# Two layers of a hybrid diffusion backbone on one core: who makes the first weight sums, where squares and spills lie, and where the modulation is computed

## The chip, the cores and the metric

The kernel runs on one core of one Trainium2 chip. The metric is device time in microseconds, as the median of several executions. The engines are TensorE (PE in the rows; its weight loads PEld), VectorE (DVE), ScalarE (ACT), GpSimd (POOL) and SyncE (SP), whose queue issues nearly all DMAs. Each engine executes its own instructions in program order, and waits for others by semaphores.

## The reference

Two layers with shared weights run over 1024 latent tokens and 256 context tokens, 1024 channels wide. Each layer does

```
mod        = silu(cond) @ w_mod[l] + b_mod[l]         # six vectors: sh1 sc1 g1 sh2 sc2 g2, per token group
h          = rms_norm(x, norm_mix[l]) * (1 + sc1) + sh1
x          = x + g1 * (mixer(h) @ w_out)              # layer 0: neighbourhood attention and pooling
                                                      # layer 1: windowed grouped-query attention
h          = rms_norm(x, norm_ffn[l]) * (1 + sc2) + sh2
gu         = h @ w_gate_up[l]
x          = x + g2 * ((silu(gu[:2816]) * gu[2816:]) @ w_down[l])
```

and a final RMSNorm follows. All of it is float32.

## The kernel before

Tokens are columns, channels are partitions. There are three blocks of columns, `TB`: ti = 0 and 1 with 512 latent tokens each, ti = 2 with the 256 prompt tokens. A float32 operand is split into two parts, a high one and the rest, and a product is three matmuls (high x high, high x rest, rest x high; L308 to L310 in `dense`, L863 to L865 in `prod`, L1032 to L1034 in `mix`). So every weight tile (`whl`, L281 copy on ScalarE, L283 subtraction) and every activation is made in two parts.

**Queue order.** The order of work is the order of the program text. Side work is put in by hand: `bg` is a list of tasks, and `bg.step(n)` issues the next n of them (a task that returns true ends the step early); `bg.need(key)` issues all up to a key. `W.done(i)` issues the making of weight unit i + 4. `md.step()` issues one step of a modulation job: eight steps are a tile of `w_mod` each (L387, L389, two products on VectorE), then two empty ones, two sums over partitions (L401, transposes on PE, and L402), and one that adds the bias. `Mod` keeps `bufs` tiles loaded ahead on SP's queue.

**Stages.** Input projection of layer 0 (up to 301 us in the trace) with modulation jobs (0, 4) to (0, 9) among it and `md.all()` at its end; attention; `out_proj`; `ffn(0)`; input projection of layer 1; attention; `out_proj`; `ffn(1)`.

**FFN.** It has 22 units (128 hidden channels each). The two latent blocks go through a seven-product scheme on 512 x 512 halves: weights G (gate) and U (up) of a unit give four weight tiles G, A, B, U, where A and B are made of sums and differences of half tiles (`make`, L272 to L276, on GpSimd), and activations give seven operands Q11, Q21, Q22, T1 to T4 (`norm_parts`). The prompt block uses plain `dense`: `prompt_gate` and `up_prompt`. Units 0 and 1 are interleaved in `begin`, since T1 to T4 are still being made there; the others are `front`, `prompt_gate`, `back`. A unit's result is split in two parts and spilled to DRAM (`spill`, tile x2_1, `hd`). Then `down(q)` goes through six groups of hidden channels (2, 4, 4, 4, 4, 4 units): `load_h` brings their spilled parts back, `mix` multiplies and adds into the residual `x` (L1036), which `load_x` has brought back from `xr`. The last group also squares the new residual and sums the squares (`Norm.feed`, ScalarE L426 into tile s2, sum L427 on GpSimd), and `tail` puts the next norm's tasks in `bg`.

**Start of the FFN.** In `out_proj` the second half (g = 1) writes the residual (L817), feeds the norm sums, and steps `bg` with the norm tasks of the block before. `norm_parts` makes the operands: `alloc` and `finish_a` (sum over partitions on PE, L433, root and reciprocal, L435 and L436), `finish_b` (L442), then, for ti = 0 and 2, `apply` (L485, L488, L491) and for ti = 1 the tasks of Q22 and T1 to T4 (L502, L503, L517, L530, L534). GpSimd or VectorE does the subtraction in `two` (L503).

## Time and profile before

| | us |
|---|---|
| median of 3 runs | 3140.95 (3139.73 to 3142.19) |
| the profiled execution | 3142.91 |
| its span, first to last instruction | 3141.1 |
| mean granted TensorE clock | 0.965 |
| PE busy | 2939.9 (94%) |
| VectorE busy | 1853.1 (59%) |
| ScalarE busy | 1090.4 (35%) |
| GpSimd busy | 852.4 (27%) |

Busy time is the time in which an engine's instructions were executing, so a PE at half clock is busy for twice as long with the same work. A wait is put down to the instruction that released it. Times in the rows are counted from the first instruction of the span.

### The profile page before, as it was taken

What the parts mean: (1) busy time and instruction counts of PE and PEld (TensorE: products, weight loads), DVE (VectorE), ACT (ScalarE), POOL (GpSimd) and SP (SyncE); (2) the same over time, 40 slices, a digit from 0 to 9 for tenths busy, and PEclk for the clock granted to TensorE, in tenths of its full rate; (3) what the DMA queues carried; (4) which work ended last, traced back from release to release, by engine and by line L of the source; (5) the groups of instructions that cost most, each with busy time, mean ns of one, the idle gap of its engine ahead of it and who ended that gap; (6) DMA issues with size and microseconds to landing.
All of it is one profiled execution on the core that took longest, in us unless ns stands there. A gap on an engine that the chain in (4) does not pass through costs nothing.

```text
span 3141.1 us, 46254 instructions
## 1 busy us (share of the span) xinstructions
PE 2939.9 (94%) x18074; PEld 2489.3 (79%) x18074; DVE 1853.1 (59%) x3007; ACT 1090.4 (35%) x2084; POOL 852.4 (27%) x720
## 2 busy tenths in 40 slices
PE   6998999969999998799989999999699999999998
PEld 4877777858888887688778778778588888888887
DVE  5655665567777777554445688872655555544334
ACT  4232674232333332000233477761433333330002
POOL 0340452233333332000222344430333343320002
PEclk9999999979999999899989999999799999999999
DMA  6458736204343445634224411123022223245421
GB/s 240 151 188 254 172 80 195 93 26 134 128 134 131 128 131 198 227 131 181 73 89 158 151 56 47 35 64 112 27 97 91 91 91 100 105 164 208 175 101 68
DMA packets 184330, 394.55 MB, mean 126 GB/s; under 512 B 32176, under 2 KB 69424, under 8 KB 177840
## 3 DMA queue, kind: packets, MB, share of 16 engines
q1 hardware_dynamic: 180656, 385.34, 36.4%
q0 software_dynamic: 3456, 6.26, 0.8%
q8 instruction: 143, 2.34, 0.3%
q14 instruction: 75, 0.61, 0.1%
HBM read 274.32 MB, written 118.23 MB: 125 GB/s over the span
## 4 chain that ended last, share of the span: by engine, by line
PE 74%; DVE 10%; ACT 5%; POOL 4%; issue 3%; DMA 3%; SPq 0%; POOLq 0%; DVEq 0%; ACTq 0%
PE psd L309 8%; PE psd L308 8%; PE psd L310 8%; PE psd L863 6%; PE psd L864 6%; PE psd L865 6%; PE psd L1032 6%; PE psd L1033 6%; PE psd L1034 6%; PE ps_t L672 5%; PE ps_o L688 4%; PE ps_s L620 4%; DVE nacc L389 2%; ACT whl L281 1%; ACT sT L677 1%
## 5 line engine op out<-in xcount | busy, mean ns | idle before, releaser
L308 PE MATMUL psd<-A,whl 128*128 128x256 f32 (+1 forms) x1760 | 586.3, 333 | 8.6 <-ACT whl L281 3.3
L309 PE MATMUL psd<-A,whl 128*128 128x256 f32 (+1 forms) x1760 | 580.9, 330 | 9.9 <-DVE A L491 9.5
L310 PE MATMUL psd<-A,whl 128*128 128x256 f32 (+1 forms) x1760 | 578.8, 329 | 1.6 <-DVE whl L283 1.6
L281 ACT ACTIVATE whl<-wraw 128x1024 fp32r<-128x1024 f32 x178 | 187.5, 1055 | 665.0 <-PE psd L1034 479.6
L1032 PE MATMUL psd<-A,whl 128*128 128x512 f32 (+1 forms) x1056 | 378.6, 359 | 30.9 <-DVE x L1036 30.8
L1033 PE MATMUL psd<-A,whl 128*128 128x512 f32 (+1 forms) x1056 | 376.0, 356 | 0.0
L1034 PE MATMUL psd<-A,whl 128*128 128x512 f32 (+1 forms) x1056 | 375.9, 356 | 0.0
L309 PEld LDWEIGHTS psd<-A,whl 128*128 128x128 f32 x1760 | 338.4, 192 | 45.5 <-DVE A L491 11.0
L308 PEld LDWEIGHTS psd<-A,whl 128*128 128x128 f32 x1760 | 338.1, 192 | 43.2 <-ACT whl L281 4.1
L310 PEld LDWEIGHTS psd<-A,whl 128*128 128x128 f32 x1760 | 342.1, 194 | 31.3 <-DVE whl L283 2.9
L1036 DVE SCALAR_TENSOR_TENSOR x<-psd,modv,x 128x512 f32<-128x512 f32 (+1 forms) x288 | 187.7, 661 | 300.8 <-PE psd L1034 283.8
L283 DVE TENSOR_TENSOR whl<-wraw,whl 128x1024 fp32r<-128x1024 f32 x174 | 235.8, 1358 | 145.5 <-ACT whl L281 143.0
L427 POOL TENSOR_TENSOR nacc<-nacc,s 128x512 f32<-128x512 f32 (+1 forms) x78 | 89.4, 1147 | 837.0 <-ACT s L426 833.7
L863 PE MATMUL psd<-A,whl 128*128 128x512 f32 x704 | 279.4, 397 | 0.0
L865 PE MATMUL psd<-A,whl 128*128 128x512 f32 x704 | 277.4, 394 | 0.0
L864 PE MATMUL psd<-A,whl 128*128 128x512 f32 x704 | 277.3, 394 | 0.0
L1032 PEld LDWEIGHTS psd<-A,whl 128*128 128x128 f32 x1056 | 201.0, 190 | 61.2 <-DVE x L1036 33.4
L662 POOL TENSOR_SCALAR sP<-sP,sm 128x896 f32<-128x896 f32 (+2 forms) x206 | 180.2, 879 | 244.7 <-DVE sm L655 118.1
L1034 PEld LDWEIGHTS psd<-A,whl 128*128 128x128 f32 x1056 | 202.1, 191 | 28.1
L1033 PEld LDWEIGHTS psd<-A,whl 128*128 128x128 f32 x1056 | 201.1, 190 | 27.5
L672 PE MATMUL ps_t<-ident,sP 128*128 128x128 f32 x1408 | 207.3, 286 | 6.2 <-POOL sP L662 2.6
L672 PEld LDWEIGHTS ps_t<-ident,sP 128*128 128x128 f32 x1408 | 153.3, 143 | 56.4 <-issue 24.9
(212 smaller groups left out, 5210.4 us busy)
## 6 DMA issues: line engine op xcount, KB each, us to landing
hd<-x SPq DMA_DIRECT2D x88, 512.0 KB, 3.1
A<-hd SPq DMA_DIRECT2D x20, 2048.0 KB, 11.0
wraw<-in_w_gu_dram SPq DMA_DIRECT2D x60, 512.0 KB, 3.6
st<-in_w_mod_dram SPq DMA_DIRECT2D x96, 256.0 KB, 2.8
wraw<-in_w_down_dram SPq DMA_DIRECT2D x44, 512.0 KB, 3.7
wmod<-in_w_mod_dram SPq DMA_DIRECT2D x64, 256.0 KB, 3.0
wrawx<-in_w_gu_dram SPq DMA_DIRECT2D x28, 512.0 KB, 3.7
A<-hd SPq DMA_DIRECT2D x14, 1024.0 KB, 15.0
```

The source lines that it names most:

```text
L281: act.activation(h[:, 0], src, AF.Copy)
L283: eng.tensor_tensor(h[:, 1], src, h[:, 0].bitcast(F32), op=OP.subtract)
L308: pe.matmul(ps[:, :n], wh, A[ti].part(0, k), start=(k == 0), stop=False)
L309: pe.matmul(ps[:, :n], wh, A[ti].part(1, k), start=False, stop=False)
L310: pe.matmul(ps[:, :n], wl, A[ti].part(0, k), start=False, stop=(k == 7))
L672: pe.transpose(pt[:, 128 * (i - lo):128 * (i - lo) + 128], P[u][:, 128 * j:128 * j + 128], ident)
L863: pe.matmul(pt, wh, t(0, c), start=(c == 0), stop=False)
L864: pe.matmul(pt, wh, t(1, c), start=False, stop=False)
L865: pe.matmul(pt, wl, t(0, c), start=False, stop=(c == 3))
L1032: pe.matmul(pt[:, :n], wh, t[:, 0, k], start=(k == 0), stop=False)
L1033: pe.matmul(pt[:, :n], wh, t[:, 1, k], start=False, stop=False)
L1034: pe.matmul(pt[:, :n], wl, t[:, 0, k], start=False, stop=(k == nk - 1))
```

## The change

Nine edits, in the order of the diff:

- `padl` and most of `ones` go, and one slab gets a longer pad.
- `make`: units up to number 13 (A and B of the first two units of an FFN) take their sums on VectorE, the rest stays on GpSimd.
- `Norm.feed`: a square can lie in a tile that the caller names. `squares` names the tiles ea and ec of the pool gq, in `out_proj` (blocks 1 and 2) and in the last group of `down`.
- `norm_parts`: a subtraction that VectorE does is issued behind the next task (`lagged`), and an empty task follows each kind.
- `out_proj`: with g = 1 only the first two of the prompt block's steps call `W.done`; `md` steps also for g = 1, ti = 0; three tasks per step rather than four; another interleaving of what is left with the prompt block's norm tasks. `begin` splits units 10 and 11 after each `front` and steps `bg` by 3 after each `prompt_gate`.
- The last unit spills into tiles wrawx and T2, takes T4's product (`c21`) ahead of Q22's, loads block 0's residual right behind it, and block 2's ahead of its `prompt_gate`. The first group of `down` takes the blocks in the order 2, 1, 0.
- The last two of the eight sums of squares in the last group go to VectorE.
- Modulation: the input projection of layer 0 keeps jobs (0, 4) to (0, 7); (0, 8) and (0, 9) move to `out_proj`, (0, 10) and (0, 11) from there to `ffn(0)`, (1, 10) and (1, 11) from `ffn(0)` to `ffn(1)`, which had none.
- The norm tasks behind `ffn(0)` get 4, 7 and 0 empty tasks in front rather than 1 each.

```diff
@@ make
-            g = self.raw.get(r)
+            g, add = self.raw.get(r), dve if self.ns < 14 else pool
...
-                pool.tensor_tensor(src[:, 512:1024], u[:, 0:512], u[:, 512:1024], op=OP.add)
-                pool.tensor_tensor(src[:, 0:512], g[:, 0:512], src[:, 512:1024], op=OP.subtract)
+                add.tensor_tensor(src[:, 512:1024], u[:, 0:512], u[:, 512:1024], op=OP.add)
+                add.tensor_tensor(src[:, 0:512], g[:, 0:512], src[:, 512:1024], op=OP.subtract)
...
@@ Norm
-        def feed(self, xc, eng=pool):
+        def feed(self, xc, eng=pool, square=None):
...
-                s = npool.tile([128, 512], F32, name="s2", bufs=3)
+                s = square() if square else npool.tile([128, 512], F32, name="s2", bufs=3)
...
@@ norm_parts
+        late = []
+        def lagged(f):
+            prev = late[:]
+            del late[:]
+            f()
+            for g in prev:
+                g()
         def two(hi, lo, src, eng=pool):
             act.activation(hi, src, AF.Copy)
-            eng.tensor_tensor(lo, src, hi.bitcast(F32), op=OP.subtract)
+            f = lambda: eng.tensor_tensor(lo, src, hi.bitcast(F32), op=OP.subtract)
+            late.append(f) if eng is dve else f()
...
@@ out_proj
+    def squares(gq):
+        n = [0]
+        def f():
+            n[0] += 1
+            return gq.tile([128, 512], F32, name=("ea", "ec")[n[0] % 2], bufs=2)
+        return f
...
-                    if ti == 2:
+                    if ti == 2 and (g == 0 or j < 2):
                         W.done(wi)
-                    if md is not None and g == 0:
+                    if md is not None and (g == 0 or ti == 0):
...
-                    bg.step((5, 5, 4 if j else 1)[ti])
+                    bg.step((5, 5, 3 if j else 1)[ti])
...
-                        bg.q = t[:1] + q[:1] + t[1:2] + q[1:2]
-                        q, t = q[2:], t[2:]
+                        bg.q = q[:1] + t[:1] + q[1:3] + t[1:2]
+                        q, t = q[3:], t[2:]
                         while q or t:
-                            bg.q += t[:2] + q[:1]
+                            bg.q += q[:1] + t[:2]
@@ ffn
         def spill(i, ti, src):
-            h = xp.tile([128, 2, 512], F32R, name="x2_1")
+            if i < NHC - 1:
+                h = xp.tile([128, 2, 512], F32R, name="x2_1")
+            elif ti == 0:
+                h = gq.tile([128, 2, 512], F32R, name="wrawx")
+            else:
+                h = gq.tile([128, 2, 4, 512], F32R, name="T2")[:, :, 0]
...
             for i in range(2):
                 front(i, S[i])
+                W.split(10 + i)
             for i in range(2):
                 prompt_gate(i, S[i])
+                bg.step(3)
...
             if last:
                 load_x(1)
+            if last:
+                c21(i, s, uw, v)
+                load_x(0)
             m = prod(w, 512, "Q22")
...
-                        for ti in range(3):
+                        for ti in ((0, 1, 2) if q else (2, 1, 0)):
                             mix(q, m + k, ti, w, 128 * GROUPS[q] * k, None)
...
-                nm.feed(xc)
+                nm.feed(xc, pool if m < 6 else dve, sq)
...
                 load_h(0, 1)
+                load_x(2)
...
-        load_x(0)
-        load_x(2)
...
-    md = Mod(st_pool, [(0, j) for j in range(4, 10)], 4)
+    md = Mod(st_pool, [(0, j) for j in range(4, 8)], 4)
...
-    md = Mod(mp, [(0, 10), (0, 11)], 3, mp)
+    md = Mod(mp, [(0, 8), (0, 9)], 3, mp)
...
-    md = [(1, j) for j in range(12)]
+    md = [(0, 10), (0, 11)] + [(1, j) for j in range(10)]
...
-        norm_tasks(nm, lambda c: xt[ti][c], 1, 0, ti, A1, (1, 1))
+        norm_tasks(nm, lambda c: xt[ti][c], 1, 0, ti, A1, ((4, 1), (7, 1), (0, 1))[ti])
...
-    ffn(W, 1, xt, A, g2, tail1, None, xr)
+    ffn(W, 1, xt, A, g2, tail1, [(1, 10), (1, 11)], xr)
```

## Rows read from the trace of the kernel before

**Rows 1.** The page: 40 slices, PE's busy tenths and its granted clock in tenths
```profile
PE   6998999969999998799989999999699999999998
...

```

**Rows 2.** Waits of PE: waiter <- releaser: us in total, times, longest us
```profile
PE psd L433 <- DVE nacc L427: 55.6, 5, 19.1
PE psd L401 <- DVE nacc L389: 30.9, 6, 12.5
PE psd L1032 <- DVE x L1036: 30.8, 6, 12.6
```

**Rows 3.** Windows: us; PE, PEld, DVE, ACT, POOL busy (x); PE clock; DMA share; GB/s
```profile
301.70:316.20 14.50, 2.00 (x10) 1.58 (x9) 13.81 (x22) 0.00 (x0) 2.66 (x3) 0.62 0.83 282
633.30:682.80 49.50, 20.26 (x79) 15.68 (x77) 34.17 (x51) 20.85 (x36) 21.17 (x17) 0.70 0.05 16
764.95:776.30 11.35, 6.01 (x29) 6.00 (x29) 7.21 (x10) 3.91 (x6) 3.44 (x3) 0.70 0.30 95
1238.20:1294.70 56.50, 32.28 (x140) 25.98 (x140) 29.18 (x45) 4.47 (x6) 0.14 (x1) 0.76 0.77 278
1284.00:1287.00 3.00, 3.00 (x9) 2.32 (x8) 3.00 (x5) 0.00 (x0) 0.00 (x0) 0.50 0.29 87
1340.00:1360.00 20.00, 20.00 (x107) 17.31 (x106) 11.60 (x17) 1.06 (x1) 0.00 (x0) 1.00 0.42 143
1565.10:1608.90 43.80, 28.44 (x150) 25.55 (x150) 18.49 (x31) 15.40 (x26) 18.72 (x14) 0.77 0.27 82
2230.00:2282.40 52.40, 24.62 (x104) 19.72 (x103) 36.17 (x54) 21.70 (x37) 21.20 (x17) 0.70 0.05 15
2815.00:2849.50 34.50, 27.86 (x134) 23.12 (x133) 18.78 (x28) 3.94 (x5) 0.00 (x0) 0.90 0.94 348
```

**Rows 4.** Timeline, 295 to 316 us: start us, us, instructions [idle before <- releaser]
```profile
302.28 2.66 POOL L1378 TENSOR_TENSOR gb<-maskb,G 128x384 f32<-128x384 bf16 x3 [4.49 <-DMA maskb<-in_mask_a_dram]
305.54 9.35 DVE L389 SCALAR_TENSOR_TENSOR nacc<-wmod,cond_raw,nacc 128x512 f32<-128x512 f32 x14
```

**Rows 5.** Waits of VectorE from 633.3 to 682.8 us
```profile
DVE whl L283 <- ACT whl L281: 7.3, 2, 5.1
DVE A L491 <- ACT A L488: 3.1, 5, 0.8
DVE nacc L427 <- POOL nacc L427: 2.7, 1, 2.7
```

**Rows 6.** The same stretch: groups (busy us, mean ns), timeline; last, the page's loads
```profile
L517 DVE SCALAR_TENSOR_TENSOR s<-x,shd,x 128x512 f32<-128x512 f32 x4 | 4.0, 996 | 0.0
L530 DVE TENSOR_TENSOR x<-x,x 128x512 f32<-128x512 f32 x4 | 3.1, 764 | 0.1
L503 DVE TENSOR_TENSOR x<-s,x 128x512 fp32r<-128x512 f32 x1 | 0.7, 692 | 0.8 <-ACT x L502 0.8
...
641.78 1.06 ACT L281 ACTIVATE whl<-st 128x1024 fp32r<-128x1024 f32 x1 [3.46 <-POOL st L273]
660.87 1.27 POOL L503 TENSOR_TENSOR A<-x,A 128x512 fp32r<-128x512 f32 x1 [4.48 <-ACT A L502]
661.49 1.20 DVE L503 TENSOR_TENSOR T<-x,T 128x512 fp32r<-128x512 f32 x1 [0.69 <-ACT T L502]
...
wraw<-in_w_gu_dram SPq DMA_DIRECT2D x60, 512.0 KB, 3.6
```

**Rows 7.** Turn to the down projection of layer 0: timeline, and windows
```profile
1280.85 1.42 DVE L389 SCALAR_TENSOR_TENSOR nacc<-st,cond_raw,nacc 128x512 f32<-128x512 f32 x2 [13.24 <-DMA st<-in_w_mod_dram]
...
1248.00:1254.00 6.00, 0.00 (x0) 0.00 (x0) 3.24 (x4) 1.58 (x2) 0.00 (x0) 0.73 0.56 172
```

**Rows 8.** Turn into layer 1: waits of VectorE from 1550 to 1600 us, and GpSimd's timeline
```profile
DVE s L453 <- POOL nacc L427: 7.1, 5, 3.0
...
1596.44 2.35 POOL L283 TENSOR_TENSOR whl<-wraw,whl 128x1024 fp32r<-128x1024 f32 x1 [2.56 <-ACT whl L281]
```

More of the change, by code (lines that the diff above doesn't have):

```diff
@@ L147, in hybrid_step @@
     padr.tile([128, 16], F32, name="pad")
-    consts.tile([128, 8], F32, name="padl")
     ident = consts.tile([128, 128], F32, name="ident")
     sp.dma_start(ident, I["ident"])
-    ones = consts.tile([128, 64], F32, name="ones")
+    ones = consts.tile([128, 8], F32, name="ones")
     dve.memset(ones, 1.0)
@@ L175, in slab @@
         pad = SHIFT if ti == 2 else 0
-        t = p.tile([128, 8 * n + (64 if pad else 0)], F32R, name=f"A{ti}{j}")
+        t = p.tile([128, 8 * n + (128 - 64 * j if pad else 0)], F32R, name=f"A{ti}{j}")
         return t[:, pad:pad + 8 * n].rearrange("p (i c n) -> p i c n", i=2, c=4)
@@ L271, in make @@
                 src = self.st
-                pool.tensor_tensor(src[:, 512:1024], u[:, 0:512], u[:, 512:1024], op=OP.add)
-                pool.tensor_tensor(src[:, 0:512], g[:, 0:512], src[:, 512:1024], op=OP.subtract)
+                add.tensor_tensor(src[:, 512:1024], u[:, 0:512], u[:, 512:1024], op=OP.add)
+                add.tensor_tensor(src[:, 0:512], g[:, 0:512], src[:, 512:1024], op=OP.subtract)
             elif kind == "B":
-                pool.tensor_tensor(g[:, 0:512], g[:, 0:512], u[:, 0:512], op=OP.subtract)
-                pool.tensor_tensor(g[:, 512:1024], g[:, 512:1024], self.st[:, 0:512], op=OP.add)
+                add.tensor_tensor(g[:, 0:512], g[:, 0:512], u[:, 0:512], op=OP.subtract)
+                add.tensor_tensor(g[:, 512:1024], g[:, 512:1024], self.st[:, 0:512], op=OP.add)
             if self.ns == 0 and self.early is not None:
@@ L525, in q22 @@
             high(c + 4)
-            low(c + 4)
+            late.append(lambda: low(c + 4))
         def first(c):
@@ L545, in fourth @@
             two(*t4[c], t, pool if c % 2 else dve)
-        return [("Q22", 0, f) for f in tasks] + [(k, 0, lambda c=c, f=f: f(c)) for k, f in (
-            ("Q22", q22), ("T1", first), ("T2", second), ("T3", third), ("T4", fourth)) for c in range(4)]
+        tasks = [("Q22", 0, f) for f in tasks]
+        for k, f in (("Q22", q22), ("T1", first), ("T2", second), ("T3", third), ("T4", fourth)):
+            tasks += [(k, 0, lambda c=c, f=f: lagged(lambda: f(c))) for c in range(4)]
+            tasks += [(k, 0, lambda: lagged(lambda: None))]
+        return tasks
     class Unit:
@@ L818, in out_proj @@
                     if g == 1:
-                        nms[ti].feed(x[ti][j])
-                        nms[ti].feed(xc, dve if j == 3 else pool)
+                        sq = g2 and squares(g2[0])
+                        nms[ti].feed(x[ti][j], pool, sq)
+                        nms[ti].feed(xc, dve if j == 3 else pool, sq)
                     sp.dma_start(xr[ti][:, u, :], xc)
-                    if ti == 2:
+                    if ti == 2 and (g == 0 or j < 2):
                         W.done(wi)
-                    if md is not None and g == 0:
+                    if md is not None and (g == 0 or ti == 0):
                         md.step()
                         md.step()
-                    bg.step((5, 5, 4 if j else 1)[ti])
+                    bg.step((5, 5, 3 if j else 1)[ti])
                 if g == 1:
@@ L894, in front @@
             act.activation(a, m, AF.Copy)
-            bg.step(6 if i else 2)
+            bg.step(5 if i else 3)
             mstep()
@@ L900, in front @@
             act.activation(c, c, AF.Silu)
-            bg.step(6)
+            bg.step(5)
         def prompt_gate(i, s):
@@ L1002, in back @@
                 up_prompt(i, s, uw)
-            c21(i, s, uw, v)
+                c21(i, s, uw, v)
             W.done(ui)
@@ L1037, in mix @@
             if nm is not None:
-                nm.feed(xc)
+                nm.feed(xc, pool if m < 6 else dve, sq)
             elif ti == 0:
                 mstep()
-        NQ = len(GROUPS)
+        NQ, sq = len(GROUPS), squares(gq)
         S = [{} for _ in range(NHC)]
```

## The prediction

> **What bounds the kernel now.** I read the 40 slices first: PE is busy nearly everywhere, and the slices where it or its granted clock falls lie where one stage hands over to the next [rows 1]. The waits of PE, longest first, name what it waits for there: sums of squares, modulation sums, and residual tiles in the down projection [rows 2]. Then I cut those hand-overs out as stretches and read in each what PE did, and at which clock [rows 3]. The reader should see six: the end of the input projection (14.5 us, PE busy 2.0), the start of each FFN (49.5 us with PE busy 20.3, and 52.4 with 24.6), the turn from its last unit to the down projection (56.5 us in layer 0, 34.5 in layer 1), and the turn into layer 1 (43.8 us, busy 28.4). Elsewhere PE is full at clock 1.00, so an edit pays only in these stretches; where PE comes back from a long wait, the granted clock is 0.50 for a few microseconds (the stretch from 1284 [rows 3]), which is the lower of its two levels (1.2 of 2.4 GHz), and this is part of each loss. All of it is counted against the profiled execution, 3142.9 us (span 3141.1, and 1.8 around it), which stands 2 us above the median of 3140.95; I take the differences from the one and apply them to the other.
>
> **Modulation jobs, input projection.** Six jobs of 13 steps make 78 steps; the six later groups of the loop give 10 each, 60, and the rest runs at the end, where PE waits for VectorE's chain of products, 9.35 us for fourteen of them [rows 4]. Four jobs make 52 steps and fit into the 60. Scores could then start when the last projection's bank is read, at about 302 (VectorE's last of it ends at 301.8), and the first bias tiles on GpSimd come at 302.3 to 304.9 anyway [rows 4]. So 316.2 becomes 302: **-14** (bounds -12 to -14.5). SP is past its loads of this spot earlier too, so the first values, 13 us later, find their tiles.
>
> **The same jobs elsewhere.** The output projection and layer 0's FFN keep as many jobs as before. Layer 1's FFN gets two, of which the before trace has none. The nearest rows are layer 0's: VectorE stands still for the first tile, falls behind, and PE waits 5.3 us at the first sum, then runs at half clock; that stretch lasts 11.35 us, 5.3 of them idle, and at a mean clock of 0.70 its 6.0 us of work hold some 2.4 more: 7.7 lost [rows 3]. The two jobs have the same code and the same VectorE load there, so I take 7.7 plus four sums of 0.35 us of PE: **+9** (bounds +1.4, if VectorE keeps up, to +12). In layer 0 VectorE comes out of the start of the FFN with less slack than before: **+2** (0 to +3).
>
> **Start of the FFN (each layer).** PE has done the output projection at 633.3 and has its prompt operand complete at 682.8. VectorE carries that chain: 34.2 of 49.5 us busy [rows 3], the other 15.3 us are waits, listed in [rows 5], with 2 x 0.69 and 0.8 in [rows 6]. Part by part:
> - Weight-half sums: GpSimd takes 1.27 us for 512 columns [rows 6], and VectorE then waits for ScalarE's copy of them, 7.3 us for units A0 and B0 [rows 5]. On VectorE a 512-wide two-input addition is 0.76 [rows 6], four of them 3.0, plus two waits of 1.06 for the copy [rows 6]: -7.3 + 5.1 = -2.2. A1 and B1 lie behind the prompt operand. A1 has to wait for a raw tile that B0 frees later than now, 3.6 us of load in the median [rows 6]; it is wanted some 8 us after the prompt operand, so this is covered, and would cost up to 3 without cover.
> - Late subtractions: 3.1 us [rows 5] and 1.4 us [rows 6] of waits for ScalarE go. Behind the late subtraction stand only tasks that are ready.
> - Squares in tiles of their own, and no weight tiles made while the last two blocks are normed: GpSimd's sums come in time. The wait of 2.7 goes [rows 5], and so does 1 us by which that addition was stretched (half of 0.76 is the price of its 256 columns, by [rows 6]); a wait of 0.6 for the last square stays: -3.1.
> - New order: three of the four T3 steps (0.996 each) and two T4 steps with a subtraction fall behind the prompt operand [rows 6]: -3.0 - 2.2, and -0.8 of the subtraction's wait.
> - Added waits: the root for the prompt rows stands on ScalarE behind the last T1 copy, and a table load behind it; VectorE's reciprocal and all later tasks queue behind that. I put 1.1 + 1.3, the second being about one ScalarE copy.
> Sum -2.2 - 4.5 - 3.1 - 6.0 + 2.4 = **-13.4 in each layer**. What is late next is still the prompt operand, so the rest of the stretch up to T3 keeps its length and its half clock. Bounds: -5, if VectorE's additions collide with GpSimd's, and -28, if the chain fell off PE's path (20.3 us of PE work at a mean clock of 0.70 fill 49.5, which leaves 29.2).
> The rows show such collisions: a subtraction that takes 692 ns on VectorE takes 1200 beside one on GpSimd; it starts at 661.49 and ends at 662.69, just behind GpSimd's, which ends at 662.14 [rows 6]. The Trainium skill says in "SBUF — State Buffer", "Who interferes with whom", that VectorE with two SBUF inputs and GpSimd reading SBUF exclude each other and the second waits for the whole of the first. The trace agrees, with these numbers. That speaks against moving sums to VectorE while GpSimd does T1's subtractions; it is a rival below.
>
> **Last unit and down projection.** PE first waits 11 us for residual tiles, then 12.6 us because VectorE waits 13.2 us for a modulation tile whose load stands behind residual loads and the next group's hidden state [rows 7]. At full speed PE does 107 matmuls in 20 us [rows 3]; 140 would take 26, so 30 of 56.5 us are lost in layer 0, and 9.4 of 34.5 in layer 1 (134 matmuls, 25.1). The change loads the prompt residuals one step earlier, takes the other halves as soon as T4 is used, gives the last spills tiles of their own (now the second spill waits for the first to land), and starts with the block whose tiles are there. In SP's queue the residual loads pass one spill and two modulation loads, and the early ones wait about 1 us for a spill of the unit before to land; behind them are weight loads that PE wants only after the turn. In layer 1 nothing else is in the way: VectorE reaches the first residual while PE still has free banks. **-7.5** (-4 to -9.4). In layer 0 the modulation tile still queues behind the hidden state. The DMA engines have a hole of 6 us at a share of 0.56 there [rows 7], where the mean of the whole stretch is 0.77 with its idle end in it [rows 3]; with the loads moved up into the hole I let the tile come 6 us sooner, and PE has two mixes of 1.15 us more behind it by then: **-9** (-2, if hidden state of the first group, now wanted in another order, comes late; -16).
>
> **Turn into layer 1.** VectorE waits 7.1 us in five places until GpSimd has read a shared tile [rows 8]; then the sum of squares is late twice, 6.4 and 9.0 us of PE by its trace, on the line of the first of [rows 2], the second because the last additions stand on GpSimd behind a weight split of 2.35 [rows 8]. Own tiles, the last two additions on VectorE and 4, 7 and 0 empty tasks ahead of the norms remove both: PE idles 15.4 of 43.8 us [rows 3] and loses some 5 more to half clock. The two additions cost VectorE 0.8 + 0.6 of wait each; with the norm tasks it is then some 6 us behind, and PE has eight banks, 11 us. **-18** (-12 to -20.9).
>
> **Very end.** The last addition moves from GpSimd to VectorE, which by the 512-column rows takes 0.5 less [rows 6] and half of that for 256. But VectorE now stops twice for a square, some 0.6 us each, among output multiplications that it does without a gap: **+0.5** (-0.4 to +1.5).
>
> The rest (constants, paddings, one to three background tasks fewer per call) has no row that waits for it: 0.
>
> Sum: -14 + 9 + 2 - 2 x 13.4 - 7.5 - 9 - 18 + 0.5 = **-63.8**, so 3142.9 becomes 3079, and on the median **3077**.
>
> **Rivals.**
> 1. Exclusion by GpSimd at every turn: each of the four sums ahead of the prompt operand waits for one GpSimd operation of 1.27 [rows 6], 5.1 a layer. For it: the 1200 ns rows. Against: T1's four additions had one stretched in four, 764 against 692 in the mean [rows 6]. -63.8 + 10 = -54: **3087**.
> 2. The start of the FFN is shorter than I think, since PE already works on the first parts of the prompt operand and keeps its clock; half of what lies between -13.4 and -28 comes too: **3062**.
> 3. A transfer that is hidden anyway: layer 0's down projection waits for the hidden state whatever the order, and the turn into layer 1 gives only its idle time less one wait: -63.8 + 9 + 9 = -46: **3095**.
> 4. Slower: PE waits for modulation sums. VectorE is the engine that gets sums, additions and two more jobs; a sum is issued three steps behind its last product, about half a unit or 13 us. From the point where VectorE is more than that behind, every sum stalls PE by 7.7 us as the first does. Before, six waits make 30.9 us, 12.5 of them at the end of the input projection [rows 2]. The forecast is used up by eight more; if 12 of the 28 sums of both FFNs stalled, -63.8 + 92 = +28: **3169**. Against: the loop's VectorE load per unit is unchanged.
> 5. The change does not do what it says: each removed wait is replaced by the next one in VectorE's queue, and the modulation gain is paid back: **3140**.
>
> **How the numbers follow.** Forecast 0.48 (3065 to 3089), rival 1 0.15, rival 2 0.15, rival 3 0.12, rival 4 0.06, rival 5 0.04. The range from 3048 to 3104 takes in rivals 1 to 3 with the nearer half of their terms' bounds and leaves out 4, 5 and the far ends. A measurement of this kernel can tell about 0.2% (6 us) from no change. Faster by more than that is everything but 4 and 5: 0.90; within 0.2%: 0.04; slower: 0.06.
>
> **What would show it.** PE starts scores near 302; the sum of squares of the prompt rows waits 2 to 3 us instead of 19; the prompt gate's last part ends about 13 us earlier counted from the end of the output projection; the stretch of the turn into layer 1 shrinks to about 26 us; in layer 1's down projection no wait over 2 us; in layer 0's one of 5 to 8 us on a modulation tile; a new wait of about 5 us in layer 1's third or fourth unit. Wrong it would be if VectorE waits for GpSimd inside the start of the FFN, or if modulation sums stall in many units.

## The result, and the profile after

The changed kernel takes 3090.71 us (median of four runs, 3085.32 to 3094.04), the kernel before 3140.34 beside it: a ratio of 0.9841, 95% interval 0.9824 to 0.9858. That is 49.6 us faster. The forecast was 3077, 14 us too low; the range from 3048 to 3104 holds the time. The profiled execution is 3094.0 us (span 3092.3); before it was 3142.9 (span 3141.1).

The page of the changed kernel, PE's busy tenths and granted clock in 40 slices, and then the clock of the kernel before (its busy tenths are in [rows 1]):

```profile
PE   6999999988999999899999999999789999999998
PEclk9999999989999999999999999999899999999999
```

```profile
PEclk9999999979999999899989999999799999999999
```

The dips at the starts of the feed-forward networks (slices 9 and 29, 6 tenths before, clock 7) are shallower, 8 and 7 with the clock at 8; the one at the turn into layer 1 (slice 21) has closed to 9. Slices 10 and 30, full before, now stand at 8: the loops behind those starts lose something, and the rows below show what.

Waits of PE, changed kernel (columns as in [rows 2]):

```profile
PE psd L400 <- DVE nacc L388: 30.7, 6, 9.9
PE psd L432 <- DVE nacc L426: 25.2, 7, 13.1
...
PE psd L441 <- DVE nr L435: 14.6, 8, 4.5
...
PE psd L1063 <- DVE x L1067: 10.3, 2, 6.5
PE psd L1514 <- ACT rt L1527: 6.4, 2, 5.8
PE psd L1063 <- DMA A<-hd: 6.0, 2, 5.4
```

Set beside [rows 2]: waits for sums of squares fell from 55.6 us to 25.2, those for residual tiles from 30.8 to 10.3. Waits for modulation sums did not fall at all, 30.9 before and 30.7 now: the longest moved from the end of the input projection (12.5) into layer 1's feed-forward loop (9.9). And two names are new: a copy that ScalarE makes at the turn into layer 1, and the hidden state's load.

Windows of the changed kernel, cut at the same matmuls as in [rows 3] (columns as there): start of the feed-forward network in layers 0 and 1, down projection's start in layers 0 and 1, turn into layer 1, first modulation sum in layer 0's loop and in layer 1's.

```profile
620.00:653.30 33.30, 20.34 (x78) 15.59 (x76) 29.22 (x48) 17.66 (x30) 11.68 (x9) 0.77 0.04 9
...
2190.40:2226.40 36.00, 22.34 (x103) 18.06 (x101) 31.79 (x52) 19.37 (x33) 11.76 (x9) 0.79 0.02 8
...
1219.60:1262.30 42.70, 32.42 (x134) 26.95 (x135) 22.78 (x36) 1.32 (x2) 0.00 (x0) 0.82 0.86 321
...
2774.40:2799.10 24.70, 24.70 (x132) 21.41 (x133) 17.81 (x28) 4.23 (x5) 0.00 (x0) 1.00 1.04 403
...
1533.00:1567.40 34.40, 24.08 (x148) 21.68 (x146) 25.44 (x39) 16.56 (x27) 13.06 (x9) 0.94 0.25 76
...
736.10:750.60 14.50, 6.44 (x30) 6.02 (x29) 10.37 (x14) 3.91 (x6) 3.46 (x3) 0.65 0.37 122
...
2308.00:2323.00 15.00, 5.07 (x24) 4.46 (x23) 11.56 (x13) 5.02 (x8) 3.66 (x3) 0.70 0.41 136
```

Five of the stretches are shorter than in [rows 3]: 33.3 us instead of 49.5, 36.0 instead of 52.4, 42.7 instead of 56.5, 24.7 instead of 34.5 and now without a gap, 34.4 instead of 43.8. Two are losses: the first modulation sum in layer 0 (14.5 instead of 11.35), and a stretch of 15.0 us in layer 1 with PE busy 5.07, which has no counterpart before.

Windows tell where a gap lies, not what a stage gained, since work moves across their edges. So I set the starts of the same matmul in both traces side by side, at stage borders; the difference of two borders is what the stage gained. The third column gives the same difference for those kernels of the study below that leave the stage as in the changed kernel: it shows how far executions scatter, and how large a difference means something.

| stage | forecast | changed kernel | the other kernels |
|---|---|---|---|
| start to 224 us | 0 | -4.4 | -3.0 to -6.9 |
| input projection | -14 | -13.6 | -15.3 to -15.4 |
| attention, output projection, layer 0 | 0 | +4.7 | +0.2 to +7.6 |
| start of FFN, layer 0 | -13.4 | -15.1 | -15.3 to -15.8 |
| loop of FFN, layer 0 | +2 | +4.3 | +1.9 to +4.8 |
| last unit and down projection, layer 0 | -9 | -9.0 | -5.9 to -8.7 |
| turn into layer 1 | -18 | -4.3 | -4.2 to -4.9 |
| attention, output projection, layer 1 | 0 | -2.1 | -5.4 to +0.7 |
| start of FFN, layer 1 | -13.4 | -15.9 | -15.7 to -16.3 |
| loop of FFN, layer 1 | +9 | +14.1 | +13.3 to +14.3 |
| last unit and down projection, layer 1 | -7.5 | -8.1 | -4.9 to -9.1 |
| end | +0.5 | +0.9 | +0.7 to +0.9 |

The column of the changed kernel adds to -48.5, which is the difference of the two spans but for 0.3. Two terms are off by 5 us or more, far beyond their scatter: the turn into layer 1 (13.7 us too little) and layer 1's loop (5 us too much). The experiments go to these first. The stages with attention scatter by several us between executions of the same code there; no weight is put on them.

The three places that the experiments start from, in the timeline of the changed kernel (start us, us, instruction [idle before <- releaser]). First layer 1's loop, VectorE and PE:

```profile
2285.28 0.88 DVE L386 TENSOR_SCALAR nacc<-st,cond_raw 128x512 f32<-128x512 f32 x2 [4.44 <-DMA st<-in_w_mod_dram]
...
2318.68 1.41 DVE L388 SCALAR_TENSOR_TENSOR nacc<-st,cond_raw,nacc 128x512 f32<-128x512 f32 x2
...
2319.48 1.11 PE L400 MATMUL psd<-ident,nacc 128*128 128x128 f32 x4 [9.93 <-DVE nacc L388]
```

VectorE waits for the first modulation tile, as forecast, and comes to the last product of the first job at 2318.7; PE had reached the sum that needs it 9.9 us earlier.

Second, the turn into layer 1, PE, ScalarE, GpSimd and VectorE:

```profile
1538.73 0.95 PE L432 MATMUL psd<-ones,nacc 128*128 128x1 f32 x8
...
1542.29 1.04 ACT L280 ACTIVATE whl<-wraw 128x1024 fp32r<-128x1024 f32 x1
...
1543.84 1.04 ACT L280 ACTIVATE whl<-wraw 128x1024 fp32r<-128x1024 f32 x1
...
1545.10 0.24 ACT L434 ACTIVATE nr<-psd,eps 128x4 f32<-128x4 f32 x1
...
1545.69 0.90 PE L441 MATMUL psd<-ident,nr 128*128 128x128 f32 x4 [4.50 <-DVE nr L435]
...
1551.14 2.39 POOL L282 TENSOR_TENSOR whl<-wraw,whl 128x1024 fp32r<-128x1024 f32 x1
...
1551.47 2.35 DVE L426 TENSOR_TENSOR nacc<-nacc,ea 128x256 f32<-128x256 f32 x1 [1.79 <-ACT ea L425]
...
1566.75 0.58 ACT L1527 ACTIVATE rt<-psd 128x512 f32<-128x512 f32 x1
...
1567.38 0.90 PE L1514 MATMUL psd<-ident,rt 128*128 128x128 f32 x3 [5.82 <-ACT rt L1527]
```

PE no longer waits for the sum of squares (L432, 1538.7). It waits for the root of it, 4.5 us, which stands on ScalarE behind two weight copies; and later 5.8 us for a copy that stands on ScalarE behind the norm's own copies. A VectorE addition of 256 columns that elsewhere takes 0.42 us ends with GpSimd's split beside it, after 2.35.

Third, the start of layer 0's down projection, SP's queue and PE:

```profile
1213.19 0.57 SPq L905 DMA_DIRECT2D A<-hd  x1
...
1219.60 0.55 PE L1063 MATMUL psd<-A,whl 128*128 128x256 f32 x1 [5.36 <-DMA A<-hd]
```

The hidden state of the prompt rows, the first that PE now wants, is the last of the three loads to be issued.

### The profile page after: what moved, and what is told of

The parts are those of the page before. It is cut to its first block, busy times and chain, and to the rows that moved or that the text cites. A ratio compares the mean times of both kernels' runs of the same rounds, so it can differ in the third digit from the quotient of the medians.

```text
span 3092.3 us, 46174 instructions
## 1 busy us (share of the span) xinstructions
PE 2937.8 (95%) x18074; PEld 2489.7 (81%) x18074; DVE 1875.6 (61%) x3035; ACT 1089.3 (35%) x2084; POOL 822.8 (27%) x692
## 4 chain that ended last, share of the span: by engine, by line
PE 68%; DVE 11%; ACT 5%; issue 3%; POOL 3%; DMA 2%; SPq 0%; DVEq 0%; ACTq 0%; POOLq 0%
PE psd L1063 6%; PE psd L1065 6%; PE psd L1064 6%; PE psd L307 6%; PE psd L309 6%; PE psd L308 6%; PE psd L884 6%; PE psd L885 6%; PE psd L886 6%; PE ps_t L684 5%; PE ps_o L700 5%; PE ps_s L632 4%; DVE nacc L388 2%; ACT whl L280 2%; DVE whl L282 2%
## 5 line engine op out<-in xcount | busy, mean ns | idle before, releaser
L1063 PE MATMUL psd<-A,whl 128*128 128x512 f32 (+1 forms) x1056 | 378.1, 358 | 16.3 <-DVE x L1067 10.3
L1063 PEld LDWEIGHTS psd<-A,whl 128*128 128x128 f32 x1056 | 201.1, 190 | 45.5 <-DVE x L1067 11.1
L426 POOL TENSOR_TENSOR nacc<-nacc,ec 128x512 f32<-128x512 f32 (+1 forms) x32 | 34.7, 1084 | 623.2 <-ACT ec L425 621.8
```

Of the source, the lines that this page charges most:

```text
L1063: pe.matmul(pt[:, :n], wh, t[:, 0, k], start=(k == 0), stop=False)
```

## Experiments

Each is the changed kernel with the edit shown; e8 and e12 join several. Times are medians of four runs with the ratio to the kernel before, run on the same chip; stages are read by the starts of the same matmuls, as in the table, since single stages move by less than the 4 us or so by which medians scatter.

### Layer 1's loop: the first modulation sum (e1_sum_later, e9_sums_later_l1)

```diff
-  self.pending = [None, None, lambda: self.sum(acc[0], v, 0), ...
+  self.pending = [None] * (2 + self.lag * (self.pos == 8)) + [lambda: self.sum(acc[0], v, 0), ...
```

e1_sum_later: `self.lag` is 4 in the feed-forward loops, and `self.pos == 8` lets it count for the first job of each loop alone.

> The changed kernel, with the first modulation sum of each layer's feed-forward loop issued four steps later. In the changed kernel PE stands 9.9 us before that sum in layer 1 and 8.1 us in layer 0, and the whole move of two jobs into layer 1 cost 12 to 15 us instead of 9. Theory A: the loss is this one wait, because VectorE is more than three steps behind its products at the first sum and the sum stands right behind PE's matmuls. Then both waits fall below 2 us, and the time falls by 12 to 18 us with the half clock behind them, to about 3073 to 3079 by the median of 3090.7. Theory B: VectorE is short of time through the whole loop; then the next sums inherit the wait, the waits at sums together stay near 31 us and the time stays within 4 us of the changed kernel.

3086.29 us, ratio 0.9827 (0.9811 to 0.9842). PE's waits in layer 1's loop, 2250 to 2480 us, changed kernel and then this one:

```profile
PE psd L400 <- DVE nacc L388: 9.9, 1, 9.9
```

```profile
PE psd L400 <- DVE nacc L388: 3.3, 1, 3.3
PE psd L309 <- DVE whl L282: 1.5, 1, 1.5
```

The wait of 9.9 us left the first sum, and 3.3 us of it reappeared at the second job's sum: VectorE was still behind. Layer 1's loop cost 9.2 us instead of 14.1. Neither theory holds alone: the wait is real, and part of it is inherited. In layer 0 the loop and the down projection together gave -10.2 where the changed kernel gave -4.8 and the other kernels -3.4 to -7.0: some 3 to 7 us gained.

e9_sums_later_l1: `[None] * (2 + self.lag)`, with 4 for both jobs of layer 1 and 0 in layer 0.

> The changed kernel, with every modulation sum of layer 1's feed-forward loop issued four steps later (two jobs), layer 0 as it is. With only the first job's sums later, the first sum's wait of 9.9 us went, but the second job's sum then waited 3.3 us and the loop kept 3.4 to 4.8 us of the gain of 11.8. Theory A (VectorE runs about 10 us behind through the first units, and whatever sum comes first pays for it once): no wait over 1.5 us at any sum in layer 1, the loop 7 to 11 us shorter, and of the 12 to 15 us that the two jobs cost there 3 to 6 stay. Theory B (VectorE's lag is paid by PE in any case, at banks or at products): other waits of PE appear in the loop, over 4 us together, and less than 5 us is gained.

3081.03 us, ratio 0.9815 (0.9801 to 0.9830). In the same stretch:

```profile
PE psd L309 <- DVE whl L282: 1.4, 1, 1.4
PE psd L886 <- DVE whl L282: 0.3, 1, 0.3
```

No modulation wait is left. The loop cost 4.3 us instead of 14.1: 9.8 us gained, theory A. VectorE has time enough in this loop; it was only late at the point where the first sums stood.

### The move of the modulation jobs as a whole (e10_jobs_before)

```diff
-  Mod(st_pool, [(0, j) for j in range(4, 8)], 4)
+  Mod(st_pool, [(0, j) for j in range(4, 10)], 4)
   (jobs 10 and 11 back in the output projection, twelve of layer 1
    in layer 0's loop, none in layer 1's)
```

> The changed kernel, with the modulation jobs placed as before: six in the input projection, two in the output projection, twelve in layer 0's feed-forward loop, none in layer 1's. Prediction: moving them is worth -14 in the input projection, +9 in layer 1 and +2 in layer 0, so undoing them loses 3 us. Theory A (the trace of the changed kernel: -14 there, +12 to +15 in layer 1, +2 to +3 in layer 0): scores start near 312 instead of 298, layer 1's loop has no modulation wait, and the time is the same within 4 us. Theory B (part of what layer 1 lost is run-to-run or comes from the start of its feed-forward network, not from the jobs): layer 1's loop gives back less than 8 us, and the undone kernel is 5 us or more slower.

3085.96 us, ratio 0.9835 (0.9812 to 0.9857): not slower than the changed kernel (0.9824 to 0.9858), its median 4.8 us lower. PE waits again at the end of the input projection, 225 to 330 us:

```profile
PE psd L400 <- DVE nacc L388: 12.2, 1, 12.2
```

That stage gains 0.4 us instead of 13.6, and layer 1's loop costs 0.0 instead of 14.1. Theory A: what the move saved in one place it paid in the other. As made, the move is worth nothing. With the sums of e9 it keeps some 11 us by these two stages; by the medians e9 is 4.9 us ahead of this kernel, and the intervals overlap, since in the two traces the stages with attention differ by 8 us the other way.

### The turn into layer 1 (e3_split_vector, e4_root_later, e8_turn_both, e5_spaces_before, e11_low_scalar)

e3_split_vector puts the four weight splits of the turn on VectorE:

```diff
-  (118, 119, 120, 121))
+  ())
```

> The changed kernel, with the four weight splits of the turn into layer 1 on VectorE instead of GpSimd. GpSimd takes 2.35 us for each, VectorE 1.23. Theory A (GpSimd is what spoils the turn): a VectorE addition waits 1.9 us behind a split, and ScalarE stands 3.6 us for a weight load that can only start when GpSimd has read its tile; without them the two PE waits of 4.5 and 5.8 us shrink together by 4 to 8 us. Theory B (the wait of 4.5 us is the root of the second half's norm, queued on ScalarE behind VectorE's backlog): the first wait stays or grows by up to 2 us, since VectorE has 4 x 1.23 us more, and the time is within 3 us of the changed kernel, or up to 3 us above.

e4_root_later puts four more empty tasks between the second half's sum and the use of its root:

```diff
-  ((4, 1), (7, 1), (0, 1))[ti]
+  ((4, 1), (7, 5), (0, 1))[ti]
```

> The changed kernel, with four more empty background tasks between the sum of squares of the second half and the use of its root in the turn into layer 1, so two mixes of the down projection lie between them. Theory A (PE stands 4.5 us because the root's round trip over ScalarE and VectorE stands behind VectorE's backlog): the wait of 4.5 us shrinks to under 2.5, and the later wait of 5.8 us, which follows from it because VectorE starts the second half's products late, changes by less than 2 either way: 2 to 4 us less in all. Theory B (VectorE's products are what sets the end of the turn, since they start later now): the first wait goes, the second grows by as much, and the time is the same within 1 us in the trace of that stretch.

e8_turn_both has both edits.

> The changed kernel with both edits to the turn into layer 1: the four weight splits on VectorE, and the root of the second half's norm used four empty tasks later. Alone, the later root took the first wait from 4.5 to 1.6 us and left the second at 6.0; the splits on VectorE took the second from 5.8 to 2.9 and raised the first to 8.8. Theory A (two separate causes: VectorE's backlog ahead of the reciprocal, and GpSimd's splits ahead of additions that VectorE waits for): together first under 3.5 and second under 3.5 us, the turn 4 to 8 us shorter than in the changed kernel. Theory B (one cause, VectorE's work between the two norms, 4 x 1.23 us more now): the first wait stays above 5 us, and the turn is no shorter than with the later root alone (3.5 to 4.5 us).

Waits of PE from 1500 to 1600 us, in this order e3, e4, e8:

```profile
PE psd L441 <- DVE nr L435: 8.8, 1, 8.8
PE psd L1514 <- ACT rt L1527: 3.5, 2, 2.9
```

```profile
PE psd L1514 <- ACT rt L1527: 6.6, 2, 6.0
PE psd L441 <- DVE nr L435: 1.6, 1, 1.6
```

```profile
PE psd L441 <- DVE nr L435: 5.8, 1, 5.8
PE psd L1514 <- ACT rt L1527: 0.6, 1, 0.6
```

| kernel | us | ratio (95%) | gain of the turn |
|---|---|---|---|
| changed | 3090.71 | 0.9841 (0.9824 to 0.9858) | -4.3 |
| e3_split_vector | 3089.07 | 0.9840 (0.9826 to 0.9855) | -2.0 |
| e4_root_later | 3085.63 | 0.9832 (0.9818 to 0.9847) | -8.7 |
| e8_turn_both | 3083.51 | 0.9825 (0.9811 to 0.9840) | -10.2 |

The splits on GpSimd alone are not it: without them the turn is 2.3 us longer. VectorE has more work ahead of the reciprocal (theory B): in e3's trace ScalarE, with the root still to do, stands idle twice for 2.0 us until VectorE's next residual. The sizes are not theory B's: the first wait grew by 4.3 us, and the second shrank by 2.9. A root that is used later is worth 4.4 us, and the second wait does not grow by it (6.0 against 5.8): theory A of that run. Both edits together give 5.9 us, but the first wait is back at 5.8, with more of the down projection done ahead of it: by the first wait that is theory B, by the second wait (0.6) and the time theory A, 1.5 us more than with the later root alone. One wait of about 6 us or more stays in every one of these kernels.

e5_spaces_before puts the empty tasks back to one ahead of each block:

```diff
-  ((4, 1), (7, 1), (0, 1))[ti]
+  (1, 1)
```

> The changed kernel, with the empty background tasks of the turn into layer 1 as before: one ahead of each block's sum of squares, instead of four, seven and none. The change gained about 6 us in this turn where 18 were forecast. Theory A (the sums' own tiles and VectorE's last two additions are what removed the waits of 6.4 and 9.0 us for sums of squares; the empty tasks only shift the norm): PE waits 1 to 3 us at one sum, and the turn is within 2 us of the changed kernel. Theory B (the empty tasks are what removed them): a wait of 5 to 7 us for the sum of squares of the second half comes back, and 3 to 6 us are lost.

3092.43 us, ratio 0.9853 (0.9834 to 0.9873); the turn gains 4.0 us instead of 4.3. Waits of PE, 1500 to 1600 us:

```profile
PE psd L432 <- DVE nacc L426: 11.4, 2, 6.9
```

This is the run that shows the mistake. With own tiles for the squares and the last two additions on VectorE, but without the empty tasks, PE still waits 11.4 us for the two sums of squares, where it waited 15.4 before. The empty tasks move the sums out of the way, and the same time comes back under two other names, 4.5 for the root and 5.8 for the copy. Of the expectation, theory B is right on the waits (6.9 us, the longest) and A on the time.

e11_low_scalar lets ScalarE write the low halves of layer 1's first norm as plain copies, so that this part of the computation is changed, and takes 24 operations from VectorE, sixteen of 512 columns, 0.66 us apart, and eight of 256:

```diff
+  if l == 1:
+      act.activation(A[ti].part(1, c - 1), t.pop(c - 1)[:, :n], AF.Identity, ...)
+  else:
       dve.scalar_tensor_tensor(A[ti].part(1, c - 1), ...
```

> The changed kernel, with the low halves of the first norm of layer 1 written by ScalarE as a plain copy instead of by VectorE as a remainder; the low halves are then not the remainders, so this part of the computation is changed. It takes 24 operations of 0.66 us from VectorE in the turn into layer 1 and gives ScalarE 24 of about 0.7. Theory A (PE's two waits of 4.5 and 5.8 us come from VectorE's backlog of norm products): both shrink, to under 5 us together, and the turn is 4 to 8 us shorter. Theory B (they come from ScalarE's queue: the root behind two weight copies, the copy of the first projected tile behind the norm's copies): with more work on ScalarE they stay or grow, and the turn is the same or longer.

3088.13 us, ratio 0.9837 (0.9816 to 0.9858); the turn is 0.3 us shorter. Waits of PE:

```profile
PE psd L1517 <- ACT rt L1530: 7.6, 2, 6.1
PE psd L441 <- DVE nr L435: 2.9, 1, 2.9
```

Some 10 us less work on VectorE (the sixteen operations) does not shorten the turn: what theory A expected does not come. The first wait lost 1.6 of its 4.5 us, the second grew. The root still stands behind the two weight copies, and the copy of the first projected tile behind the norm's copies, which are now twice as many on ScalarE: from 1552.4 us to that copy at 1561.3 ScalarE has no gap. That fits theory B. But the run moves the load from VectorE to ScalarE, so it shows neither that VectorE's work had no part in the changed kernel's second wait (there ScalarE stands idle for VectorE's scaled products, 2.0 and 0.6 us, ahead of the same copy) nor what taking the weight copies away would give.

### The order of layer 0's down projection (e2_down_order)

```diff
-  for ti in ((0, 1, 2) if q else (2, 1, 0)):
+  for ti in ((0, 1, 2) if q else (1, 2, 0)):
```

> The changed kernel, with the first down projection's blocks in the order second half, prompt, first half instead of prompt, second half, first half. In the changed kernel PE stands 5.4 us in layer 0 before its first down matmul, by the trace for the prompt rows of the hidden state, whose load is issued last of the three. Theory A: that load is late, so with another block first the 5.4 us go, and the time falls by 4 to 7 us (part of them may come back at the later waits for the modulation tile, 6.5 us now). Theory B: the weight copy on ScalarE, which ends only 0.7 us before that load lands, is as late, and PE then stands 4.5 to 5 us for the copy: the time falls by less than 1 us. Theory C: nothing is gained at the end of the projection because the later wait on VectorE grows by as much (to about 11 us).

3090.09 us, ratio 0.9846 (0.9830 to 0.9863). Waits of PE from 1195 to 1290 us:

```profile
PE psd L1063 <- DVE x L1067: 11.8, 2, 6.3
PE psd L1063 <- DMA A<-hd: 5.8, 1, 5.8
```

PE starts the down projection early, but then waits 5.8 us for the same load; the later waits are 11.8 us instead of 10.3. Idle in all 17.6 us against 15.7. Theory A falls; nothing is gained, as theory C has it, though the wait for the load stays too and the later ones grow by 1.5 us only.

### The start of the feed-forward network (e6_sums_gpsimd, e7_order_before)

```diff
-  g, add = self.raw.get(r), dve if self.ns < 14 else pool
+  g, add = self.raw.get(r), pool
```

> The changed kernel, with the weight-half sums of the first two units back on GpSimd, in both layers. Theory A (the prediction's term): the sums on VectorE are worth 2.2 us in each start of the feed-forward network, so this loses 2 to 3 us in each, 4 to 6 in all. Theory B (exclusion: each VectorE sum costs a GpSimd operation of 1.27 us): the sums on VectorE are worth nothing or cost up to 3 us, so this is the same or gains. Theory C (VectorE's chain has left PE's path in the changed kernel, which has gained more in this stretch in layer 1 than forecast): sums on GpSimd put VectorE's wait of 7 us for ScalarE's copy back in the chain, and 5 to 8 us are lost in each layer.

3095.06 us, ratio 0.9864 (0.9848 to 0.9880). VectorE's wait for ScalarE's weight copies from 600 to 700 us, changed kernel and then this one, and a new wait of PE in this one:

```profile
DVE whl L282 <- ACT whl L280: 10.6, 9, 2.4
```

```profile
DVE whl L282 <- ACT whl L280: 22.7, 9, 6.2
PE psd L307 <- ACT whl L280: 2.6, 1, 2.6
```

The start gains 8.9 us in layer 0 and 9.4 in layer 1, where the changed kernel gained 15.1 to 15.9: the sums on VectorE are worth 6.2 and 6.5 us by the end of this stage, three times the forecast term. By its size that is theory C; where it falls follows below.

```diff
-  bg.q = q[:1] + t[:1] + q[1:3] + t[1:2]
+  bg.q = t[:1] + q[:1] + t[1:2] + q[1:2]
   ...
-      bg.q += q[:1] + t[:2]
+      bg.q += t[:2] + q[:1]
```

> The changed kernel, with the order of the background tasks at the end of the output projection as before: prompt tasks one slot earlier, one other task behind every two of them. Theory A (the prediction's term): fewer T3 and T4 steps ahead of the prompt operand are worth 6 us in each layer, so this loses 4 to 6 us in each. Theory B: these steps are only moved and PE waits for them behind the prompt operand instead, so this loses under 1.5 us in each.

3096.94 us, ratio 0.9866 (0.9852 to 0.9881). The start gains 10.7 and 11.1 us: the order is worth 4.4 and 4.8 us by the end of this stage. By its size that is theory A.

The forecast counted both terms up to the last part of the prompt operand. The matmul that takes it, in the changed kernel, e6 and e7 (layer 0):

```profile
653.33 0.58 PE L308 MATMUL psd<-A,whl 128*128 128x256 f32 x1 [3.60 <-DVE A L490]
```

```profile
649.22 0.58 PE L308 MATMUL psd<-A,whl 128*128 128x256 f32 x1 [2.40 <-DVE A L490]
```

```profile
647.28 0.58 PE L308 MATMUL psd<-A,whl 128*128 128x256 f32 x1 [5.27 <-DVE A L490]
```

Counted from the first matmul behind the output projection (619.97, 614.47 and 613.41 us) it starts at 33.4, 34.8 and 33.9 us, where it was 49.5 before; layer 1 is the same within 0.2 us. Up to there the sums on VectorE are worth 1.4 us and the order 0.5. The rest falls some 20 us later, at the up weights of the first unit: PE waits 2.6 us for their copy in e6 and 1.8 in e7, not at all in the changed kernel, and the granted clock over the next 10 us is 0.66 and 0.83 instead of 1.00. VectorE's lines say why the order does so little for the prompt operand: of the T3 and T4 products six stood ahead of it before (5.5 us), one does in the changed kernel and none in e7, so another of the edits moved them; which one, no run here shows.

Both kernels also show where a gain at this place goes. Their layer 1 loop costs only 9.9 us instead of 14.1: PE arrives 4.8 to 6.5 us later at the first modulation sum and waits 3.6 to 4.3 us less there. In layer 0 the same wait, 8.1 us, is only 1.2 to 1.5 us shorter.

### What helped, together (e12_best)

Sums four steps later (first job of layer 0's loop, both of layer 1's), the root four empty tasks later, the splits on VectorE.

> The changed kernel with what has helped together: modulation sums four steps later (first job of layer 0's loop, both jobs of layer 1's), the root of the second half's norm four empty tasks later, the four splits of the turn on VectorE. Alone they gained about 10 us (layer 1's sums), 3 (layer 0's first sum) and 4 (the turn). If they add, 17 us off the changed kernel: about 3074. If layer 0's gain is only moved to the down projection's wait for the modulation tile: about 3077. If the kernel is not faster than with layer 1's sums alone, 3081, the gains of the turn come back in layer 1's attention.

3072.41 us (3067.92 to 3077.74), ratio 0.9788 (0.9766 to 0.9809): 18 us faster than the changed kernel, as expected if the gains add, and the intervals do not meet. By stages layer 1's loop costs 4.3 us, the turn gains 10.4, and layer 0's loop with its down projection gains 10.2. The longest waits of PE that stay are for sums of squares (25.5 us in seven) and for modulation sums (17.2 us in five).

## Why the prediction was right or wrong

**Input projection (-14): right.** Scores start at 298.1 instead of 316.2, and the stage alone gains 13.6 us; e10 takes it back to 0.4.

**The same jobs elsewhere (+9 and +2): the place and the mechanism right, the size too small.** Layer 1's loop lost 14.1 us, beyond the bound of 12; layer 0's 4.3, beyond the bound of 3 (1.9 to 4.8 in other kernels). The step that failed is that of the nearest row: I took layer 0's wait of 5.3 us over to layer 1 "with the same VectorE load". But the wait is the difference between when PE arrives and when VectorE ends its last product, and the change itself lets PE arrive earlier, by its own gain at the start of the network. e6 and e7 show this link: 4.8 to 6.5 us less gain there, 3.6 to 4.3 us less wait here. Gains ahead of a fixed wait are partly given back at it, and my sum added them as if they were free of each other. Rival 4 had the mechanism, but as eight more stalls; it was one large one in each layer, and e9 removes layer 1's.

**Start of the feed-forward network (-13.4 in each layer): right, some 2 us too small, and not in all its parts.** It gave 15.1 and 15.9, and 16.1 where the forecast counted it, at the prompt operand. There VectorE's waits fell from 15.3 us to 4.1 and its work from 34.2 to 29.2. By its rows the waits for late subtractions (3.1 and 1.4 us) and for GpSimd's sum of squares (2.7) went as forecast; no kernel here undoes these edits, so their prices are read, not shown. The sums on VectorE came near their term (1.4 of 2.2). The step that failed here is the new order: 0.5 instead of 6.0. The T3 and T4 products did fall behind the prompt operand, but they do so with the old order too. And it had no term for what is lost behind the prompt operand without either edit, 4 to 5 us each.

Rival 1 is settled too. In layer 0 one of the four sums ahead of the prompt operand met a GpSimd operation (timeline, changed kernel):

```profile
635.41 1.28 POOL L511 TENSOR_TENSOR T<-x,T 128x512 fp32r<-128x512 f32 x1 [1.95 <-ACT T L510]
...
635.71 1.53 DVE L271 TENSOR_TENSOR st<-wraw 128x512 f32<-128x512 f32 x1
637.28 0.69 DVE L272 TENSOR_TENSOR st<-wraw,st 128x512 f32<-128x512 f32 x1
```

It took 1.53 us where the next took 0.69: 0.84 us lost once, not four times 1.27; of the four sums behind the prompt operand one more, at 664.57, took 1.78 us beside GpSimd's subtractions. Layer 1 has the same two. The rule of the Trainium skill in "SBUF — State Buffer", "Who interferes with whom", that VectorE with two SBUF inputs and GpSimd reading SBUF exclude each other, agrees with these rows (the sum ends only after GpSimd's has). But with 1.9 us a layer it takes far less than the 6.2 to 6.5 that the sums on VectorE save.

**Last unit and down projection (-9 in layer 0, -7.5 in layer 1): right.** -9.0 and -8.1. The new wait for the prompt rows' hidden state is the one that the bound named; the other order of e2 does not avoid it. This is the first half of rival 3 by its wait, but not by its price: the term gave its 9.0 all the same.

**Turn into layer 1 (-18): wrong, it gave 4.3.** The step that failed is "own tiles, the last two additions on VectorE and 4, 7 and 0 empty tasks ahead of the norms remove both", and the argument that PE has eight banks and so cannot be late. The wait for a sum of squares was the last link of a chain: residual addition, square, addition, sum, root, reciprocal, scaled product, copy, and PE needs the end of it. By e5 the first two edits shortened it by 4.0 of 15.4 us, and the third renamed the rest. Free banks were no help here, since PE waited for values that it needed itself (4.5 us for the root, 5.8 for the copy). I read who released PE, and not what would release it next. Rival 3's second half says this (the turn gives its idle time less one wait). In the window of [rows 3] its -9 is met: 43.8 us became 34.4, where the forecast had 26. But the wait for the copy stands at the end of that window, and the granted clock is 0.70 behind it: the work that PE does from there took 6.5 us before, at a clock of 1.00 (1609 to 1616 us), and takes 9.7 now. The table's -4.3 holds that too. That rival 3's time, 3095, is nearer to the result than the forecast is in part luck, since its other half did not come.

What makes up the rest of the turn stays open in part. It is not GpSimd's splits alone (e3), and taking work from VectorE is no help where ScalarE gets it (e11); the distance between the sum and the use of its root counts (e4, 4.4 us). That the weight copies ahead of the root on ScalarE are the next link is read from the timelines and not shown, since no kernel here moved them away, and they cannot be all of it: the two take 2.1 of the 5.4 us between the end of the sum and the root, and squares, a norm copy and gaps take the rest.

**End (+0.5): right,** +0.9.

Against the sum of -63.8, 15 us are missing by the profiles: 13.7 at the turn, 5.1 in layer 1's loop, 2.3 in layer 0's, 2.6 in the stages with attention, less 4.2 that the two starts gave in addition and 4.4 ahead of 224 us, where the change does nothing that I know of. Two terms lie well beyond their bounds, and the range holds the time all the same; the 8.6 us that came without being counted helped, and that is luck.

## What to carry to other kernels

When a wait is to be removed, write down the whole chain from that wait to the value that the waiting engine needs next, and ask at each link what it would then wait for; a delay put in front of a wait (empty tasks, another order) changes its name before it changes the time. A sum that one engine issues and another must have finished should stand as many steps behind its last input as that engine lags in the worst unit, and the lag has to be taken after the other gains of the same change, since every gain ahead of it makes the waiting engine arrive earlier. Moving work from one stage to another was here two terms of similar size and opposite sign, and deserves a kernel of its own (e10) before it is called a gain. And a kernel that undoes an edit is to be read where the forecast counted the term, not only at the end of the stage: e7 gave back 4.4 us in layer 0, but 0.5 at the place of the term of 6.0.

## What was not expected of the hardware

A weight split on GpSimd takes 2.35 to 2.39 us, and a VectorE addition that runs into it pays most of that, 1.93 us: 2.35 us for 256 columns that take 0.42 alone. And the clock costs more than the idle time shows: behind the wait of 9.9 us in layer 1's loop the granted clock is 0.58 over the next 5.5 us, near the lower of its two levels (1.2 of 2.4 GHz), and behind the one of 5.8 us in the turn 0.70 over 7 us: the 24 matmuls there take 7.68 us by their starts and ends, and 24 of the same form some 25 us later take 5.73. The two windows, of the changed kernel, columns as in [rows 3]:

```profile
2319.50:2325.00 5.50, 5.50 (x29) 5.50 (x30) 3.27 (x5) 0.64 (x1) 2.96 (x3) 0.58 0.19 48
...
1569.00:1576.00 7.00, 7.00 (x23) 5.64 (x24) 0.17 (x1) 0.88 (x3) 0.00 (x0) 0.70 0.75 226
```
